# Which half chunk of the next block's weights GpSimd splits at the mixer's norm, in a decoder trunk on one Trainium2 core

## The chip, the cores and the metric

The kernel runs on one core of a Trainium2 chip. The metric is the device time of one execution in microseconds (us). Three runs of the kernel before took 1212.08, 1212.16 and 1212.49 us; their median is 1212.16.

The engines are named as in the profile: PE is TensorE (matmuls; PEld is its weight load), DVE is VectorE, ACT is ScalarE, POOL is GpSimd, and SP is SyncE, which issues most of the transfers. L180 means line 180 of the kernel.

## The reference, cut to what matters

The reference computes two layers, each with three blocks, and a layer norm behind each block. Activations are 256 tokens by 1024 features, all in float32.

```python
for l in range(DEPTH):                       # DEPTH = 2
    h = _swiglu(x, ffn_w1[l, 0], ffn_w3[l, 0], ffn_w2[l, 0])
    x = _layernorm(ALPHA * x + 0.5 * h, ln_g[l, 0], ln_b[l, 0])
    h = _mixer(x, l, w_in[l], ...)           # ends with: m @ w_out
    x = _layernorm(ALPHA * x + h, ln_g[l, 1], ln_b[l, 1])
    h = _swiglu(x, ffn_w1[l, 1], ffn_w3[l, 1], ffn_w2[l, 1])
    x = _layernorm(ALPHA * x + 0.5 * h, ln_g[l, 2], ln_b[l, 2])

def _swiglu(x, w1, w3, w2):                  # d_ff = 2816
    return (jax.nn.silu(x @ w1) * (x @ w3)) @ w2
```

The mixer is a gated pair of branches (a spatial gating unit and a differential attention), whose sum `m` goes through `w_out`. The change touches the passage from that last product, over the layer norm behind it, into the first products of the second SwiGLU of the same layer. There is one such passage in each layer, so two in all.

## The kernel before

**Products in three matmuls.** Each float32 operand is held as a hi part (rounded to the format that the matmul reads) and a lo part (what the rounding left). A product is three matmuls into one accumulator: hi weights by hi x, lo weights by hi x, hi weights by lo x (`three`, L256 is its matmul). The profile names the parts `whi`, `wlo` for weights and `x` for both parts of the new x (`mhi`, `mlo` for the operand of `w_out`).

**Weights come in chunks.** `stream` (L152) fetches one chunk of weights, 128 partitions by 2048 float32 (1 MB), by one transfer of SyncE's queue into a `raw` buffer (L163; there are four). The chunk falls into two half chunks, and each half into two pieces of 128x512. For each piece ScalarE makes the hi part (L178) and another engine makes the lo part by subtracting it from the raw weights (L180). That engine is VectorE, except for the half chunks that the argument `pool` names, which go to GpSimd. The hi and lo buffers for half chunks come from two pools of eight each; they become free as TensorE reads the last matmul of the half chunk that held them. `lent` names half chunks that are put into spare activation buffers instead (`lhi`, `llo`), so that they can be split before the pools have room.

**The first products of a block.** `gemm_b2` (L317) multiplies the 256 tokens, as two halves of 128 (t = 0 and 1), by two weight matrices (m = 0 and 1) of 512 columns each, over 8 row tiles of 128 (c = 0 and 1 hold four each). That makes four chunks n = 2c + m. For t = 0 each is fetched, split and used for 12 matmuls; for t = 1 the same four are used again. The order of a chunk's use in t = 0 is n = 0, 1, 2, 3. Chunks 0 and the first half of 1 are lent. The second half of 1, and all of 2 and 3, are in the pools.

**The norm between.** The block before a norm ends with `gemm_b2` for `w_out`, whose first token half is complete 48 matmuls ahead of its second. `Norm.part` (L467, and L471 for statistics) adds the residual; `Norm.finish` aggregates (L478), takes a reciprocal root in one-element steps (`rsqrt`, L228 to L234), normalises the two halves of the features (L487, two pieces of 128x512), and writes the second one as two 16-bit planes (L526) for a transposing transfer. All of this is on VectorE. TensorE transposes the first feature half itself (L533). `affine` then applies the norm's gain and bias on ScalarE (L580), and `split` makes the hi and lo parts of the new x (L220 on ScalarE, L222 on VectorE; on GpSimd for the second feature half of the first tokens). The next block's first matmul needs x's parts.

**What sets the order.** TensorE's program is in the order written. The other engines' order comes from a scheduler that goes by priorities; `behind(ins)` puts an instruction behind another in that order, and the lists `after` and `lent` and the argument `pool` of `gemm_b2` are written out for the passage. `norm.ends[0]` is the last plane (L526) of the first token half, and `norm.ends[1]` that of the second. `norm.front` is the index of the norm in its layer: it is 1 only for the norm behind the mixer.

In the kernel before, at a passage behind the mixer, GpSimd makes the lo parts of the second half of chunk 2; VectorE makes the others. VectorE's lo parts for the second half of chunk 1 and the first half of chunk 2 stand behind the planes of the first token half; chunk 3's stand behind those of the second token half.

Of the kernel before, what the change touches and what calls it, by code (L numbers as in the profile page):

```python
# [54 lines left out]
def trunk(ctx, tc, x, xT, w13a, w13b, w2, wb, wqk, wu, wg, wgr, wbr, wbrr, wo, gateb, gatebr, sgug, sgub, sguwT, sgubias, lam, diffg,  # L55
# [22 lines left out]
    def bank():  # L78
        return psum.tile([P, 512], F32, tag="main", name=name("bank"))
# [68 lines left out]
    def behind(ins):  # L148

        return tc.issue_after(ins) if ins is not None else nullcontext()  # L150

    def stream(src, width=CH, sub=HC, lent=(), after=(None, None), pool=()):  # L152

        step()
        raw = raw_pool.tile([P, CH], F32, tag="raw", name=name("raw"))
        for g in gate:
            g[0] -= 1
        while len(gate) > 1 and gate[1][0] < 0:  # L160
            gate.pop(0)
        with behind(gate[0][1] if gate and gate[0][0] < 0 else None):
            loaded[0] = nc.sync.dma_start(raw[:, :width], src).ins  # L163
        out = []
        first = sooner.pop() if sooner else latest
        for o in range(0, width, HC):
            eng = G if o // HC in pool else V
            if o // HC in lent:
                hi, lo = ([act.tile([P, 512], F32R, tag="slot", name=name(n)) for _ in range(2)] for n in ("lhi", "llo"))
                at = [(hi[j], lo[j]) for j in range(2)]  # L170
            else:
                hi = hi_pool.tile([P, HC], F32R, tag="hi", name=name("whi"))
                lo = lo_pool.tile([P, HC], F32R, tag="lo", name=name("wlo"))
                at = [(hi[:, p : p + sub], lo[:, p : p + sub]) for p in range(0, HC, sub)]
            for p, (h, w) in zip(range(0, HC, sub), at):
                r = raw[:, o + p : o + p + sub]
                with behind(first[0]):
                    A.activation(h, r, AF.Copy)  # L178
                with behind(after[o // HC] or (first[1] if eng is V else None)):
                    eng.tensor_tensor(out=w, in0=r, in1=h.bitcast(F32), op=ALU.subtract)  # L180
            out.append((hi, lo))
        return out
# [104 lines left out]
    def rows_b(ps, t, k0, piece, xh, xl, kts, c0=0, n=512, first=0):  # L287

        hi, lo = piece
        for j in range(2):  # L290
            k, o = k0 + j, j * 512 + c0
            wh, wl = (w[j][:, c0 : c0 + n] if isinstance(w, list) else w[:, o : o + n] for w in (hi, lo))
            three(ps[:, :n], xh(k)[:, t * P : (t + 1) * P], xl(k)[:, t * P : (t + 1) * P], wh, wl,
                  k == first, k == (first - 1) % kts)
        beat(n / 1024)
# [21 lines left out]
    def gemm_b2(srcs, xh, xl, done, norm=None, second=(0, 1), each=None):  # L317

        lent, after = [()] * 4, [(None, None)] * 4
        if norm:
            lent = [(0, 1), (0,), (), ()]
            after[1:3] = (None, norm.ends[0]), (norm.ends[0], None if norm.front == 1 else norm.ends[0])
        ps = [[bank() for _ in range(2)] for _ in range(NT)]
        got = [[None] * 4 for _ in range(2)]
        for t in range(NT):
            order = second if t else (0, 1)
            for c in order:
                if norm:  # L330
                    norm.ready(t, c)
                    after[3] = [norm.ends[1]] * 2
                for m in range(2):
                    n = 2 * c + m
                    if t == 0:
                        got[m][2 * c : 2 * c + 2] = stream(srcs[m][:, c * CH : (c + 1) * CH], sub=512, lent=lent[n],
                                                           after=after[n], pool=(1,) if norm and norm.front == 1 and n == 2 else ())
                    for i in range(2 * c, 2 * c + 2):
                        rows_b(ps[t][m], t, 2 * i, got[m][i], xh, xl, KT, first=order[0] * KT // 2)
                    if each and c == order[1]:  # L340
                        each(t, m, ps[t][m])
            with behind(latest[0] if t == 0 else None):
                done(t, ps[t])
# [255 lines left out]
    def ffn(l, f, i, norm, last=False):  # L599
# [33 lines left out]
        for n in range(NB):  # L633
            srcs = [w13b[l, f, m * NB + n] for m in range(2)]
            if n == 0 and norm is None:
                gemm_first(srcs, front(n, (10.3, 10.3)))
            else:
                gemm_b2(srcs, xh, xl, front(n, (13.3, 10.3)), norm=norm if n == 0 else None)
# [17 lines left out]
    def mixer(l, i, norm):  # L656
# [5 lines left out]
        def got_val(t, ps):  # L662
            for h in range(2):
                with behind(norm.xhi[1, 0]):
                    A.activation(val[t][:, h], ps[h], AF.Copy)

        gemm_b2([wb[l, VAL_, 0], wb[l, VAL_, 1]], xh, xl, got_val, norm=norm)

        hb = slots("hb", 2 * KT, F32R)
# [273 lines left out]
        for c, m in branch_columns(0, ha, ((0,), (1,))):  # L943
# [3 lines left out]
        ln = Norm(l, i, 2.0 * ALPHA, 4.0 * EPS, m[:, :1])  # L947

        gemm_b2([wo[l, 0], wo[l, 1]], view(m_hi), view(m_lo), lambda t, ps: ln.finish(t, 1.9), second=(1, 0),
                each=lambda t, h, ps: ln.part(t, h * 512, ps))  # L950
        return ln.close()

    norm = None
    for l in range(DEPTH):
        norm = ffn(l, 0, 0, norm)
        norm = mixer(l, 1, norm)
        norm = ffn(l, 1, 2, norm, last=l == DEPTH - 1)
# [87 lines left out]
```

## Time and profile before

| | before |
|---|---|
| median of three runs | 1212.16 us |
| the profiled execution | 1212.03 us |
| its span, first to last instruction | 1210.3 us |
| granted TensorE clock | 1.000 |
| PE busy | 1203.2 us (99% of the span) |
| PEld busy | 1012.9 us (84%) |
| DVE busy | 905.2 us (75%) |
| ACT busy | 720.1 us (59%) |
| POOL busy | 334.9 us (28%) |

Busy time is the time in which an engine's instructions ran, whether or not anything waited for them. The chain of work that ended last is the view that tells what sets the end: it is followed back from the last instruction to what released it, step by step. In rows of the timeline the first number is the start from the span's beginning and the second the length of the row; "x2" means two instructions merged into one row, and the bracket at the end is the idle time of the engine just before the row, with what ended it. Two instructions of one engine may overlap by some hundredths of a microsecond, as the next is taken up while the last drains.

### The profile page before, as it was taken

The numbers are of one execution on the slowest core, as the hardware profiler recorded it, in microseconds if no ns is written. First come the engines' busy times: TensorE is split into PE (matmuls) and PEld (weight loads), VectorE is DVE, ScalarE is ACT, GpSimd is POOL, SyncE is SP. The second block draws the span as 40 slices with busy tenths as digits, with TensorE's granted clock in tenths as the row PEclk, the third lists the DMA queues.
The fourth block names the chain that finished last, engine by engine and source line by source line (L and its number), as shares of the span: only waits on it lengthen the run. The fifth ranks groups of instructions, "written<-read, shape, count | busy, mean of one in ns | idle before, by whom it ended". The sixth has DMA issues, their size and how long they took to land.

```text
span 1210.3 us, 16816 instructions
## 1 busy us (share of the span) xinstructions
PE 1203.2 (99%) x5891; PEld 1012.9 (84%) x5891; DVE 905.2 (75%) x1544; ACT 720.1 (59%) x1388; POOL 334.9 (28%) x442
## 2 busy tenths in 40 slices
PE   9999999999999999999999999999999999999998
PEld 8888888888888888888888888888888887888887
DVE  7676669897688986766686766688976989776763
ACT  7465547668855665554555564576698556564740
POOL 1433101156411233330053330003564012423300
PEclk9999999999999999999999999999999999999999
DMA  9977746767765566766476757476676764877540
GB/s 348 301 224 234 251 174 205 261 198 229 239 218 183 191 235 204 252 197 260 148 246 200 259 183 261 148 273 232 213 217 194 250 191 146 276 230 239 186 180 35
DMA packets 124005, 263.58 MB, mean 218 GB/s; under 512 B 88416, under 2 KB 89488, under 8 KB 97808
## 3 DMA queue, kind: packets, MB, share of 16 engines
q1 hardware_dynamic: 119664, 248.80, 61.6%
q0 software_dynamic: 3824, 13.18, 3.4%
q8 instruction: 46, 0.75, 0.2%
q10 hardware_dynamic: 432, 0.52, 0.1%
q14 instruction: 39, 0.32, 0.1%
HBM read 236.52 MB, written 1.05 MB: 196 GB/s over the span
## 4 chain that ended last, share of the span: by engine, by line
PE 95%; DVE 4%; issue 1%; ACT 0%; ACTq 0%
PE bank L256 69%; PE bank L268 15%; PE bank L275 7%; PE bank L374 2%; PE sbank L704 1%; DVE wlo L180 1%; PE sbank L760 1%; PE sbank L878 1%; DVE llo L180 1%; DVE st L471 0%; PE sbank L386 0%; DVE xtok L467 0%; DVE nvia L526 0%; PE sbank L758 0%; DVE mlo L222 0%
## 5 line engine op out<-in xcount | busy, mean ns | idle before, releaser
L180 DVE TENSOR_TENSOR wlo<-raw,whi 128x512 fp32r<-128x512 f32 (+1 forms) x566 | 526.0, 964 | 114.1 <-ACT whi L178 80.0
L178 ACT ACTIVATE whi<-raw 128x512 fp32r<-128x512 f32 (+1 forms) x570 | 433.3, 799 | 246.8 <-PE bank L256 181.0
L256 PE MATMUL bank<-whi,x 128*128 128x512 f32 x1480 | 460.6, 390 | 0.0
L256 PEld LDWEIGHTS bank<-whi,x 128*128 128x128 f32 x1480 | 277.9, 188 | 57.8
L256 PE MATMUL bank<-wlo,x 128*128 128x512 f32 x740 | 288.0, 389 | 0.0
L256 PEld LDWEIGHTS bank<-wlo,x 128*128 128x128 f32 x740 | 139.0, 188 | 28.1
L268 PE MATMUL bank<-x,whi 128*128 128x512 f32 x640 | 153.3, 391 | 0.0
L193 POOL COPY planes<-planes 128x512 uint16<-128x512 uint16 x80 | 90.4, 1157 | 190.9 <-DVE planes L613 190.9
L256 PE MATMUL bank<-whi,hhi 128*128 128x512 f32 (+1 forms) x374 | 141.2, 378 | 0.0
L256 PE MATMUL bank<-wlo,hhi 128*128 128x512 f32 (+1 forms) x374 | 141.0, 377 | 0.0
L256 PE MATMUL bank<-whi,hlo 128*128 128x512 f32 (+1 forms) x374 | 140.9, 377 | 0.0
L268 PEld LDWEIGHTS bank<-x,whi 128*128 128x128 f32 x640 | 118.2, 188 | 23.8
L202 POOL COPY planes<-planes 128x512 uint16<-128x512 uint16 x80 | 69.5, 913 | 96.2 <-DMA planes<-planes 95.8
L613 DVE TENSOR_TENSOR planes<-planes,bank 128x512 f32<-128x512 f32 x40 | 27.3, 683 | 85.8 <-issue 70.9
L612 ACT ACTIVATE planes<-bank 128x512 f32<-128x512 f32 x40 | 23.9, 598 | 103.7 <-PE bank L256 102.2
L275 PEld LDWEIGHTS bank<-x,wlo 128*128 128x128 f32 x640 | 81.4, 191 | 2.9
L275 PE MATMUL bank<-x,wlo 128*128 128x256 f32 x640 | 82.6, 283 | 0.0
L256 PEld LDWEIGHTS bank<-whi,hlo 128*128 128x128 f32 x374 | 70.4, 188 | 13.0
L256 PEld LDWEIGHTS bank<-whi,hhi 128*128 128x128 f32 x374 | 70.4, 188 | 12.8
L256 PEld LDWEIGHTS bank<-wlo,hhi 128*128 128x128 f32 x374 | 70.4, 188 | 12.6
L575 POOL COPY nvia<-ntwo 128x256 uint16<-128x256 uint16 x20 | 10.3, 563 | 195.6 <-DMA ntwo<-nvia 177.4
L680 POOL TENSOR_TENSOR swap<-swap,sin_t 128x512 f32<-128x512 f32 x16 | 25.3, 1582 | 103.2 <-DMA swap<-z 80.6
(209 smaller groups left out, 1393.4 us busy)
## 6 DMA issues: line engine op xcount, KB each, us to landing
raw<-in_w13b SPq DMA_DIRECT2D x76, 1024.0 KB, 5.8
raw<-in_w SPq DMA_DIRECT2D x40, 1024.0 KB, 6.3
raw<-in_wb SPq DMA_DIRECT2D x16, 1024.0 KB, 5.2
raw<-in_wqk SPq DMA_DIRECT2D x16, 1024.0 KB, 6.5
raw<-in_w13a SPq DMA_DIRECT2D x8, 1024.0 KB, 5.1
raw<-in_wgr SPq DMA_DIRECT2D x8, 1024.0 KB, 5.6
raw<-in_wg SPq DMA_DIRECT2D x8, 1024.0 KB, 5.2
raw<-in_wu SPq DMA_DIRECT2D x8, 1024.0 KB, 6.4
```

Source lines behind the costliest of these rows:

```text
L178: A.activation(h, r, AF.Copy)
L180: eng.tensor_tensor(out=w, in0=r, in1=h.bitcast(F32), op=ALU.subtract)
L193: G.tensor_copy(out=planes(out)[:, w], in_=numbers(src)[:, w])
L202: eng.tensor_copy(out=numbers(out)[:, w], in_=planes(src)[:, w])
L256: PE.matmul(ps, xx, w, start=start and n == 0, stop=stop and n == 2)
L268: PE.matmul(b[-1], hi[:, k * P : (k + 1) * P], xc(k), start=k == 0, stop=False)
L275: PE.matmul(b[n][:, :T], lo[:, k * P : (k + 1) * P], xc(k)[:, :T], start=False, stop=k == KT - 1)
L374: PE.matmul(ps[t][m], x[:, j, o + t * P : o + (t + 1) * P], y, start=k0 + j == 0 and o == 0 and y is hi, stop=k0 + j == KT - 1 and y is lo)
L612: silu[0] = A.activation(s, ps[0], AF.Silu).ins
L613: added[0] = V.tensor_tensor(out=s, in0=s, in1=ps[1], op=ALU.mult).ins
L680: turned_by[0] = G.tensor_tensor(out=s3, in0=s3, in1=s, op=ALU.mult).ins
L704: PE.matmul(banks[m][:, j * nk : (j + 1) * nk], rows(qT, m, j, t * P, P), rows(kT, m, j, 0, nk), start=True, stop=True)
```

## The change

At the passage behind the mixer, GpSimd makes the lo parts of the second half of chunk 1 in place of the second half of chunk 2. They carry no order of their own: they stand where they may run as soon as their hi parts and their buffer are there. The second half of chunk 2 goes to VectorE, behind the planes of the first token half. At the other norms (`norm.front` 0 and 2) the new lists say the same as the old ones, and nothing changes.

```diff
         if norm:
             lent = [(0, 1), (0,), (), ()]
-            after[1:3] = (None, norm.ends[0]), (norm.ends[0], None if norm.front == 1 else norm.ends[0])
+            after[1:3] = (None, None if norm.front == 1 else norm.ends[0]), [norm.ends[0]] * 2
...
                     if t == 0:
                         got[m][2 * c : 2 * c + 2] = stream(srcs[m][:, c * CH : (c + 1) * CH], sub=512, lent=lent[n],
-                                                           after=after[n], pool=(1,) if norm and norm.front == 1 and n == 2 else ())
+                                                           after=after[n], pool=(1,) if norm and norm.front == 1 and n == 1 else ())
```

In the built program this moves two instructions on VectorE and two on GpSimd at each passage. VectorE's two lo parts for the second half of chunk 1, first behind the planes, are gone, and two for the second half of chunk 2 stand behind those for its first half. GpSimd's pair keeps its place in GpSimd's order, between the loads of the next norm's gain and bias (L434) and its plane copies (L575), and now reads chunk 1. TensorE's order is the same; its two matmuls with chunk 1's lo parts of that half now wait for GpSimd. ScalarE's order and SyncE's are the same.

## The prediction, made before the change was run

> **What bounds the kernel now.** I read the page's chain of work first, then the same chain in order of time, then TensorE's own rows where that chain leaves TensorE.
>
> ```profile
> PE 95%; DVE 4%; issue 1%; ACT 0%; ACTq 0%
> 398.84 0.53 issue
> ...
> 416.13 1.41 issue
> 417.54 1.84 DVE nvia L526 x2
> 419.38 2.41 DVE wlo L180 x4
> ...
> 423.11 0.60 DVE x L222
> 423.75 108.65 PE bank L256 x478
> ...
> 997.29 0.53 issue
> ...
> 1022.46 108.64 PE bank L256 x478
> ```
>
> 95% of the end is TensorE; what an edit off TensorE can win is only the time in which TensorE stands. The chain leaves TensorE for long at two places, 398.84 to 423.75 us and 997.29 to 1022.46 us: the two passages from a mixer to the FFN behind it (layers 0 and 1), which are the places this diff touches. There the norm of the first token half runs on VectorE: normalise (L487 x2), planes (L526 x2), four weight lo parts (L180 x4), then the lo part of the new x (L222), for which TensorE waits.
>
> TensorE at the first passage (columns: start, length, line, out<-in; a matmul starts when the array takes it, so steps are read from start to start):
>
> ```profile
> 417.56 0.39 PE L256 MATMUL bank<-whi,mlo 128*128 128x512 f32 x1
> ...
> 418.15 0.48 PE L256 MATMUL bank<-whi,mhi 128*128 128x512 f32 x1
> ...
> 422.59 0.39 PE L256 MATMUL bank<-llo,x 128*128 128x512 f32 x1
> 423.75 0.73 PE L256 MATMUL bank<-lhi,x 128*128 128x512 f32 x2 [0.78 <-DVE x L222]
> 424.32 0.39 PE L256 MATMUL bank<-llo,x 128*128 128x512 f32 x1
> ...
> 427.52 0.39 PE L256 MATMUL bank<-whi,x 128*128 128x512 f32 x1
> ...
> 434.32 0.39 PE L256 MATMUL bank<-lhi,x 128*128 128x512 f32 x1
> ```
>
> From 427.52 to 434.32 lie 30 matmuls (6 of the ordinary half of chunk 1, 12 each of chunks 2 and 3): 6.80/30 = 0.227 us a step. From 422.59 to 424.32 lie three steps, 0.68 undisturbed, and they take 1.73: 1.05 lost. From 424.32 to 434.32 lie 44 steps, 9.97 at that rate, in 10.00: 0.03 more lost in a slow restart.
>
> The second passage:
>
> ```profile
> 1016.01 0.39 PE L256 MATMUL bank<-whi,mlo 128*128 128x512 f32 x1
> 1016.38 0.66 PE L533 MATMUL sbank<-ident,xtok 128*128 128x128 f32 x4
> 1016.79 0.48 PE L256 MATMUL bank<-whi,mhi 128*128 128x512 f32 x1
> ...
> 1021.21 0.39 PE L256 MATMUL bank<-llo,x 128*128 128x512 f32 x1
> 1022.46 0.73 PE L256 MATMUL bank<-lhi,x 128*128 128x512 f32 x2 [0.86 <-DVE x L222]
> 1023.03 0.39 PE L256 MATMUL bank<-llo,x 128*128 128x512 f32 x1
> ```
>
> Here 1021.21 to 1023.03 is 1.82, less 0.68: 1.14 lost. And the four transposes (L533) start late: 1016.01 to 1016.79 is 0.78 where the first passage has 0.59 (417.56 to 418.15), 0.19 lost waiting for the normalised half.
>
> **The change, part by part.** Chunk n is the n-th of the four weight chunks of the block; each has two half chunks, each of two 128x512 lo parts. Both kernels give GpSimd two lo parts a passage, and VectorE the rest; every engine keeps its count, ScalarE and SyncE their order, so no DMA is added or moved past another. VectorE now makes the second half of chunk 2 where it made the second half of chunk 1: same four L180 behind the planes, no cost. GpSimd's two lo parts go from chunk 2 to chunk 1. The rows that matter (L178 makes the hi parts on ScalarE):
>
> ```profile
> 412.55 1.15 ACT L178 ACTIVATE whi<-raw 128x512 fp32r<-128x512 f32 x2 [3.16 <-PE bank L256]
> ...
> 415.33 1.15 ACT L178 ACTIVATE whi<-raw 128x512 fp32r<-128x512 f32 x2 [0.22 <-PE bank L256]
> ...
> 420.42 0.64 ACT L220 ACTIVATE x<-xf 128x512 fp32r<-128x512 f32 x1
> ```
> ```profile
> 416.04 2.71 POOL L180 TENSOR_TENSOR wlo<-raw,whi 128x512 fp32r<-128x512 f32 x2 [9.48 <-ACT whi L178]
> 1014.49 2.97 POOL L180 TENSOR_TENSOR wlo<-raw,whi 128x512 fp32r<-128x512 f32 x2 [9.10 <-ACT whi L178]
> ```
>
> The first hi row is chunk 1's second half, the second chunk 2's second half (chunk 2's first is between them). GpSimd starts 0.71 behind its hi part (415.33 to 416.04) and has been idle for 9.48, so it is the hi part alone that holds it. Behind chunk 1's it starts at 412.55 + 0.71 = 413.26, 2.78 earlier, and ends 2.71 to 2.97 later, at 415.97 to 416.23.
>
> What that does to VectorE is read from the rows in which the two ran together and one in which they did not:
>
> ```profile
> 415.50 2.11 DVE L487 TENSOR_SCALAR xtok<-xtok,mv,nwy 128x512 f32<-128x512 f32 x2
> 415.97 1.65 DVE L487 TENSOR_SCALAR xtok<-xtok,mv,nwy 128x512 f32<-128x512 f32 x1
> 417.54 1.50 DVE L526 COPY nvia<-xtok 128x512 uint16<-128x512 uint16 x1
> 418.96 0.42 DVE L526 COPY nvia<-xtok 128x512 uint16<-128x512 uint16 x1
> 427.35 0.55 DVE L487 TENSOR_SCALAR xtok<-xtok,mv,nwy 128x512 f32<-128x512 f32 x1
> 427.93 0.43 DVE L526 COPY nvia<-xtok 128x512 uint16<-128x512 uint16 x1
> ```
>
> Alone (427.35, 427.93) a normalise takes 0.55 and a plane 0.43. Under GpSimd's first lo part the second normalise takes 1.65, under its second lo part the first plane 1.50, ending at 419.04, which is 0.29 after GpSimd ended (416.04 + 2.71 = 418.75). The second plane, behind it, is back at 0.42. So VectorE's wide one-input operations stand until GpSimd's is through. With GpSimd done at 415.97 to 416.23, only the first normalise (415.50) is touched: it ends 0.29 behind, at 416.26 to 416.52. The second follows 0.47 later (the spacing 415.97 - 415.50), the planes 0.46 (0.03 gap and 0.43) and 0.34 (419.38 - 419.04) later: 417.53 to 417.79, against 419.38 now, 1.6 to 1.85 earlier.
>
> The Trainium skill, "SBUF — State Buffer", section "Who interferes with whom", says that of a VectorE operation in a two-port mode and a GpSimd one, the first to issue holds the shared ports for its whole instruction and the other blocks fully; by that rule, and the trace agrees with its 1.65 and 1.50, the order matters and not the mean load.
>
> L222 moves with it from 423.11 to 421.26 to 421.51. Its hi part is ready at 420.42 + 0.64 = 421.06, so ScalarE does not hold it, and it is through 0.64 later (423.11 to 423.75), by 421.9 to 422.15. TensorE asks for it at 422.59 + 0.23 = 422.82. The wait goes wholly, with 0.7 to 0.9 to spare. The second passage has the same instructions in the same order, with GpSimd's pair 598.45 later (1014.49) and TensorE's request 598.62 later (1021.21 against 422.59): I take the same 1.6 to 1.85, more than the 1.14 lost there, and the transposes find their half, worth the 0.19.
>
> What is late next: GpSimd's lo part has a new reader, a TensorE wait, at 427.52, 11 us behind its end: nothing. Chunk 2's second half, now VectorE's, is ready about 420 and is asked for at 430.2 (427.52 and 12 steps): nothing. GpSimd's next work waits for a transpose that starts when the planes end, and comes earlier with them.
>
> Sum: 1.05 + 0.03 at the first passage, 1.14 + 0.02 (taken like the first's) + 0.19 at the second: 2.43 us. Behind both, the chain is TensorE's again (108.65 and 108.64 at one stretch), which carries the gain on. The profiled execution takes 1212.03 (span 1210.3): 1209.60. It is 0.13 below the median of the three runs, 1212.16, so I forecast 1209.7. About what a measurement of this kernel can tell from no change is 0.2%, 2.42 us, a bound at 1209.74: my sum lies on it.
>
> The cost that before does not show is VectorE's small operations (the eight one-element steps of the root, 413.45 to 415.50) beside GpSimd's 128x512 lo parts. The nearest row is GpSimd's own L222:
>
> ```profile
> 424.60 1.57 POOL L222 TENSOR_TENSOR x<-nvia,x 128x256 fp32r<-128x256 f32 x2 [1.50 <-ACT x L220]
> ...
> 425.68 0.27 DVE L233 TENSOR_SCALAR nwa<-yi,ve 128x1 f32<-128x1 f32 x1
> ...
> 413.45 0.15 DVE L228 TENSOR_SCALAR ve<-mv 128x1 f32<-128x1 f32 x1
> ...
> 413.83 0.28 DVE L233 TENSOR_SCALAR nwa<-yi,ve 128x1 f32<-128x1 f32 x1
> ```
>
> Beside GpSimd (424.60 to 426.17) the root's step takes 0.27, without it 0.28: I take nothing. The lower end is nothing too, since none of these steps waits for GpSimd now; the upper end is full blocking (third rival).
>
> **The rivals.** First, the wait comes back at the second token half, whose x is asked for at 434.32:
>
> ```profile
> 423.62 0.68 DVE L467 SCALAR_TENSOR_TENSOR xtok<-xtok,bank 128x512 f32<-128x512 f32 x1
> ...
> 434.51 0.39 ACT L220 ACTIVATE x<-nvia 128x256 fp32r<-128x256 f32 x1
> ```
>
> That half's norm begins with L467 at 423.62. Its last matmul is two steps ahead of 422.59 and through 0.39 later, at 422.5, so VectorE is what holds it and it moves up by about a microsecond too; then nothing is lost. Were something else to hold it (a transpose, ScalarE), x's third column tile, ready at 434.90, would be asked for six steps behind the earlier head, 434.32 - 1.08 + 1.36 = 434.60: 0.30 lost, and 0.57 at the second passage by the same sum with 1.35 for 1.08. That gives 1209.73 + 0.87 = 1210.6.
>
> Second, GpSimd does not start early and nothing moves: 1212.2. Against it: it idles 9.48, and its buffer belongs to the half chunk whose hi buffer came free at 412.55.
>
> Third, the other side: GpSimd's lo parts block the small steps as they block the wide ones. The eight steps (413.45 to 415.50, 2.05) would start at about 416.0 and normalise at 418.0; the two pairs, now alone, take 1.82 (0.47 + 0.55, 0.03 + 0.43 + 0.34): 419.8, 0.45 behind now. Transposes and x follow: 0.9 over both passages, 1213.1; over 1214.6 only if GpSimd's parts get longer by it as well. It decides against the change once the steps lose more than the 1.85 won. The skill's page, same section, lists tensor_scalar among those that can take the two-port mode, which speaks for it; the 0.27 speaks against.
>
> **How the numbers follow.** Forecast 0.82: 1209.5 to 1210.1, since the runs of before spread over 0.4; a little over half of it beyond the bound, 0.48 against 0.34. First rival 0.09, second 0.03, both within 0.2%. Third 0.06: 0.02 within, 0.04 beyond. Faster 0.48, same 0.48, slower 0.04. The range takes in the forecast with 0.5 below it for slow steps that I have not counted, and the first rival with as much again as it costs, 1209.0 to 1211.3; it leaves out the last two cases and little more.
>
> **What would show it.** GpSimd's L180 at about 413.3 and 1011.7; the second normalise near 0.55 and both planes near 0.43; the root's steps at 0.15 to 0.28 still; L222 at 421.3 to 421.5; TensorE from the llo matmul at 422.59 to the next in 0.23; no new wait near 433. The prediction is wrong if the root's steps grow, if a TensorE gap reappears at the second half's head, or if GpSimd's L180 still starts at 416.

## The result, and the profile after

The changed kernel took 1209.74 us in the median of 21 runs (1209.36 to 1210.40). The kernel before took 1212.42 in as many runs on the same chips (1210.73 to 1212.93), 0.26 above the three runs shown ahead of the prediction. The ratio is 0.998, with a 95% interval of 0.9973 to 0.9986: 2.68 us, 0.22%. That is just beyond the 0.2% that the prediction took as the bound, but the interval, 0.14% to 0.27%, takes the bound in. The profiled execution took 1210.00, with a span of 1208.3.

The chain of work in order of time, of the changed kernel, at the first passage and then at the second (start, length, what; the views end at 440 and 1030, and with them the last row of each):

```profile
400.58 17.71 PE bank L256 x78
418.30 0.44 PE sbank L533 x4
418.73 21.36 PE bank L256 x94
...
998.03 17.71 PE bank L256 x78
1015.74 0.44 PE sbank L533 x4
1016.18 13.88 PE bank L256 x61
```

VectorE, which carried most of this chain from 398.84 to 423.75 before, is no longer in it. TensorE's own rows at the place where it stood 1.05 us, and then at the same place of the second passage:

```profile
422.93 0.39 PE L256 MATMUL bank<-llo,x 128*128 128x512 f32 x1
423.15 0.62 PE L256 MATMUL bank<-lhi,x 128*128 128x512 f32 x2
423.61 0.39 PE L256 MATMUL bank<-llo,x 128*128 128x512 f32 x1
...
433.58 0.39 PE L256 MATMUL bank<-lhi,x 128*128 128x512 f32 x1
...
1020.37 0.39 PE L256 MATMUL bank<-llo,x 128*128 128x512 f32 x1
...
1021.05 0.39 PE L256 MATMUL bank<-llo,x 128*128 128x512 f32 x1
```

Three steps in 0.68 at both, and no gap at the head of the second token half either: 47 steps from 422.93 to 433.58, 0.227 each. What made it so, on ScalarE, GpSimd and VectorE (timeline of the changed kernel, engine by engine):

```profile
412.89 1.15 ACT L178 ACTIVATE whi<-raw 128x512 fp32r<-128x512 f32 x2 [2.77 <-PE bank L256]
...
413.61 2.55 POOL L180 TENSOR_TENSOR wlo<-raw,whi 128x512 fp32r<-128x512 f32 x2 [6.31 <-ACT whi L178]
...
414.18 0.15 DVE L228 TENSOR_SCALAR ve<-mv 128x1 f32<-128x1 f32 x1
...
416.24 1.00 DVE L487 TENSOR_SCALAR xtok<-xtok,mv,nwy 128x512 f32<-128x512 f32 x2
417.15 0.75 DVE L526 COPY nvia<-xtok 128x512 uint16<-128x512 uint16 x2
417.83 2.49 DVE L180 TENSOR_TENSOR wlo<-raw,whi 128x512 fp32r<-128x512 f32 x4
...
421.56 0.68 DVE L222 TENSOR_TENSOR x<-xf,x 128x512 fp32r<-128x512 f32 x1
422.90 0.69 DVE L467 SCALAR_TENSOR_TENSOR xtok<-xtok,bank 128x512 f32<-128x512 f32 x1 [0.67 <-PE bank L256]
```

GpSimd's pair is through at 416.16, before VectorE's first wide operation (416.24). The two normalises take 1.00 together instead of 2.11, the two planes 0.75 instead of 1.84. L222 is through at 422.24, 0.9 ahead of TensorE's request (422.93 + 0.23), and VectorE now waits 0.67 for TensorE at L467: the wait has turned round.

### The profile page after: what moved, and what is told of

Its sections match the earlier page's. It is cut to its first block, busy times and chain, and to the rows that moved or that the text cites. A ratio compares the mean times of both kernels' runs of the same rounds, so it can differ in the third digit from the quotient of the medians.

```text
span 1208.3 us, 16816 instructions
## 1 busy us (share of the span) xinstructions
PE 1202.6 (100%) x5891; PEld 1013.3 (84%) x5891; DVE 903.2 (75%) x1544; ACT 719.9 (60%) x1388; POOL 332.9 (28%) x442
## 3 DMA queue, kind: packets, MB, share of 16 engines
HBM read 236.52 MB, written 1.05 MB: 197 GB/s over the span
## 4 chain that ended last, share of the span: by engine, by line
PE 99%; DMA 0%; DVE 0%; ACT 0%; issue 0%; ACTq 0%
PE bank L256 72%; PE bank L268 15%; PE bank L275 8%; PE bank L374 2%; PE sbank L704 1%; PE sbank L760 1%; PE sbank L878 1%; DMA xraw<-in_xT 0%; PE sbank L758 0%; PE sbank L533 0%; PE sbank L512 0%; DVE xtok L520 0%; ACT whi L220 0%; DVE st L471 0%; DVE xtok L467 0%; ACT x L220 0%
## 5 line engine op out<-in xcount | busy, mean ns | idle before, releaser
L202 POOL COPY planes<-planes 128x512 uint16<-128x512 uint16 x80 | 70.9, 931 | 95.8 <-DMA planes<-planes 95.5
L575 POOL COPY nvia<-ntwo 128x256 uint16<-128x256 uint16 x20 | 10.4, 565 | 198.1 <-DMA ntwo<-nvia 179.9
```

What stands on the lines that cost most here:

```text
L202: eng.tensor_copy(out=numbers(out)[:, w], in_=planes(src)[:, w])
```

## The experiments

The theory: VectorE's wide operations stand while GpSimd's weight lo parts run; the change takes GpSimd out of their way, and TensorE gets back what it lost there. The main rivals: it is VectorE's load that counts, or the choice of the half chunk as such. Each kernel below is timed against the kernel before on the same chip, which took 1212.38 us in the median beside the first four below and 1212.63 beside the others.

**GpSimd takes no lo parts.** VectorE makes all six behind the planes.

```diff
-            after[1:3] = (None, None if norm.front == 1 else norm.ends[0]), [norm.ends[0]] * 2
+            after[1:3] = (None, norm.ends[0]), [norm.ends[0]] * 2
...
-   pool=(1,) if norm and norm.front == 1 and n == 1 else ())
+   pool=())
```

> GpSimd makes no weight lo parts at the two passages; VectorE makes all six behind the planes, two more than in either kernel. Theory (VectorE's wide one-input operations stand while GpSimd works; with the overlap gone they take 0.55 and 0.43): the planes end as early as in the changed kernel, two more lo parts cost 1.2 us, L222 ends about 0.3 behind TensorE's request, so a stall of 0.3 to 0.4 a passage: 1210.3 to 1210.6 us. Rival (what counts is the load on VectorE, and GpSimd's help shortens the chain): two more lo parts on the chain put x 1.2 us later than before at each passage: about 1214.8 us.

Measured: 1210.36 us, ratio 0.9984 (0.9975 to 0.9993). VectorE, then TensorE, in its timeline:

```profile
415.94 1.00 DVE L487 TENSOR_SCALAR xtok<-xtok,mv,nwy 128x512 f32<-128x512 f32 x2
416.86 0.76 DVE L526 COPY nvia<-xtok 128x512 uint16<-128x512 uint16 x2
417.53 3.69 DVE L180 TENSOR_TENSOR wlo<-raw,whi 128x512 fp32r<-128x512 f32 x6
...
422.47 0.68 DVE L222 TENSOR_TENSOR x<-xf,x 128x512 fp32r<-128x512 f32 x1
...
422.64 0.39 PE L256 MATMUL bank<-llo,x 128*128 128x512 f32 x1
423.20 0.73 PE L256 MATMUL bank<-lhi,x 128*128 128x512 f32 x2 [0.17 <-DVE x L222]
423.77 0.39 PE L256 MATMUL bank<-llo,x 128*128 128x512 f32 x1
```

VectorE does 1.2 us more than in the kernel before and x comes earlier all the same; TensorE loses 1.13 - 0.68 = 0.45 here, and as much at the second passage. In the kernel before, GpSimd's help cost more than the work it took over. The rival's 1214.8 is out.

**GpSimd works on into the old time.** As the changed kernel, with its two lo parts made twice.

```diff
+            if eng is G:
+                for p, (h, w) in list(zip(range(0, HC, sub), at))[:again]:
+                    G.tensor_tensor(out=w, in0=raw[:, o + p : o + p + sub], in1=h.bitcast(F32), op=ALU.subtract)
             out.append((hi, lo))
...
-   pool=(1,) if norm and norm.front == 1 and n == 1 else ())
+   pool=(1,) if norm and norm.front == 1 and n == 1 else (), again=2)
```

> As the changed kernel, but GpSimd makes its two lo parts of chunk 1 a second time into the same buffer, so that it works on from 416.2 to about 418.7 as it did before. Theory: the second normalise (or the first) and the first plane stand again, the planes end near 419.7, the whole wait of TensorE is back: 1212.0 to 1212.8 us. Rival (the gain comes from which half chunk goes to GpSimd: its hi parts, its buffers): nothing comes back, 1209.6 to 1209.9 us.

Measured: 1212.20 us, ratio 1.0 (0.9991 to 1.0009). GpSimd, VectorE and TensorE (its lines stand three later, L490 for L487):

```profile
416.06 2.71 POOL L183 TENSOR_TENSOR wlo<-raw,whi 128x512 fp32r<-128x512 f32 x2
...
416.19 2.87 DVE L490 TENSOR_SCALAR xtok<-xtok,mv,nwy 128x512 f32<-128x512 f32 x2
418.99 0.75 DVE L529 COPY nvia<-xtok 128x512 uint16<-128x512 uint16 x2
...
417.85 0.39 PE L259 MATMUL bank<-whi,mlo 128*128 128x512 f32 x1
419.12 0.66 PE L536 MATMUL sbank<-ident,xtok 128*128 128x128 f32 x4 [0.87 <-DVE xtok L490]
419.53 0.48 PE L259 MATMUL bank<-whi,mhi 128*128 128x512 f32 x1
```

The gain is gone with the half chunk unchanged, so the half chunk as such wins nothing. This time both normalises stand and no plane, and TensorE loses its time at the transposes (419.53 - 417.85 = 1.68 where 0.59 is undisturbed, 1.09) instead of at x, where 0.05 is left: nearly the same delay, asked for elsewhere.

**Half of that.** The same with `again=1`.

> As the changed kernel, but GpSimd makes one of its two lo parts a second time, so that it works to about 417.5. Theory: one wide operation stands, about 1.1 us on VectorE's chain, of which 0.9 is the slack that the changed kernel has at L222; 0.2 to 0.3 of stall with the restart a passage: 1210.1 to 1210.5 us. Rival (each blocked operation costs its full length, no slack): 2.1 us for both passages, about 1211.9 us.

Measured: 1210.12 us, ratio 0.9982 (0.9973 to 0.9991).

```profile
416.10 1.48 POOL L183 TENSOR_TENSOR wlo<-raw,whi 128x512 fp32r<-128x512 f32 x1
...
415.73 2.14 DVE L490 TENSOR_SCALAR xtok<-xtok,mv,nwy 128x512 f32<-128x512 f32 x2
```

The normalises take 2.14 for 1.00, the 1.1 us expected, and the rival's 1211.9 is out: the slack takes it up. TensorE shows no long step at the first passage in this profile and 0.15 at the second (0.70 for 0.59 at the transposes, 0.72 for 0.68 at x), less than the 0.2 to 0.3 expected at each. The median stands 0.38 above the changed kernel's; 0.15 of it is read here, and the rest, inside this run's interval of about 1.1 us to each side, stays open.

**The first passage alone, the second alone.** The norm keeps its layer, and the change is made only where the layer is 0 (shown), or 1.

```diff
+            if norm.front == 1 and norm.layer != 0:
+                after[1:3] = (None, norm.ends[0]), (norm.ends[0], None)
+            else:
+                after[1:3] = (None, None if norm.front == 1 else norm.ends[0]), [norm.ends[0]] * 2
...
+   pool=(1,) if norm and norm.front == 1 and n == (1 if norm.layer == 0 else 2) else ())
```

> The change at the first passage alone, the second as before. Theory: the first passage's 1.08 us of the 2.43 are won, 1211.3 us against 1212.4; TensorE's long step stays at the second passage and is gone at the first. Rival (the two passages share one cause further on and only both together win anything): 1212.4 us, with a new wait behind the first passage.

Measured: 1210.97 us, ratio 0.9991 (0.9982 to 0.9999), 1.41 won where 1.08 was counted.

> The change at the second passage alone. The first passage alone won 1.4 us where 1.08 had been counted from the profile of before. Theory: the profile of before caught VectorE early at its first passage (GpSimd's copies L202 near 399 us held it less than in the later profiles), so the usual loss there is about 1.4; the second passage then wins the rest of 2.68, about 1.3: 1211.1 us, and this run's own first passage shows a loss of 1.3 to 1.5 us. Rival (the two passages do not add up, winning one makes the other smaller): 1211.3 us or more, and the first passage loses 1.05 as in the profile of before.

Measured: 1211.07 us, ratio 0.9989 (0.9980 to 0.9998). Against the 1212.4 that this expectation reckoned with that is 1.3; against its own chip's 1212.63 it is 1.56. The two passages together give 2.7 to 3.0 for the 2.68 of the whole change. Each of the two times has an interval of about 1.1 us to each side, so they can't separate the expected 1211.1 from the rival's 1211.3; the traces do. TensorE at the unchanged first passage of this run:

```profile
417.38 0.39 PE L256 MATMUL bank<-whi,mlo 128*128 128x512 f32 x1
...
418.16 0.48 PE L256 MATMUL bank<-whi,mhi 128*128 128x512 f32 x1
...
422.56 0.39 PE L256 MATMUL bank<-llo,x 128*128 128x512 f32 x1
423.83 0.73 PE L256 MATMUL bank<-lhi,x 128*128 128x512 f32 x2 [0.88 <-DVE x L222]
424.40 0.39 PE L256 MATMUL bank<-llo,x 128*128 128x512 f32 x1
```

Read as in the prediction: 1.84 - 0.68 = 1.16 at x and 0.78 - 0.59 = 0.19 at the transposes, 1.35 where the first profile had 1.05. At the changed second passage nothing is lost. In the run with the first passage changed it is the other way round: nothing at the first, 1.36 at the second.

**The kernel before, profiled again.**

> The kernel before once more, for a second profile of it. Theory: the losses of TensorE at the passages are not fixed; at the first one 1.3 to 1.5 us where the first profile had 1.05, at the second 1.3 to 1.5. Rival: 1.05 and 1.33 again, and the 0.25 us by which the measured gain passes the counted one comes from elsewhere.

One run, 1213.04 us. TensorE at its first passage:

```profile
418.20 0.39 PE L256 MATMUL bank<-whi,mlo 128*128 128x512 f32 x1
...
418.99 0.48 PE L256 MATMUL bank<-whi,mhi 128*128 128x512 f32 x1
...
423.43 0.39 PE L256 MATMUL bank<-llo,x 128*128 128x512 f32 x1
...
425.24 0.40 PE L256 MATMUL bank<-llo,x 128*128 128x512 f32 x1
```

0.20 and 1.13, 1.33. Read the same way, the unchanged second passages of three profiles show 1.33 (the first profile), 1.36 (this one) and 1.36 (the first passage alone changed). So the first profile's first passage, with 1.05, was the odd one of six. The two first passages differ already 20 us earlier. In this profile GpSimd's copies (L202) hold VectorE's pair of lo parts and the next operation, 0.5 each; in the first one they came earlier and the pair alone was held, 0.64 (1.29 is the pair's time undisturbed, below):

```profile
400.33 2.12 POOL L202 COPY gr<-gr 128x512 uint16<-128x512 uint16 x2 [6.29 <-ACT whi L178]
...
400.02 1.81 DVE L180 TENSOR_TENSOR wlo<-raw,whi 128x512 fp32r<-128x512 f32 x2 [0.53 <-issue]
401.75 1.19 DVE L222 TENSOR_TENSOR mlo<-gate,mhi 128x512 fp32r<-128x512 f32 x1
```

The first profile of the kernel before:

```profile
398.93 1.89 POOL L202 COPY gr<-gr 128x512 uint16<-128x512 uint16 x2 [5.45 <-DMA gr<-gr]
...
399.38 1.93 DVE L180 TENSOR_TENSOR wlo<-raw,whi 128x512 fp32r<-128x512 f32 x2 [0.53 <-issue]
401.23 0.68 DVE L222 TENSOR_TENSOR mlo<-gate,mhi 128x512 fp32r<-128x512 f32 x1
```

In the second profile the root's first step (L228) comes 1.03 later (414.48 for 413.45) and TensorE's last matmul before its wait 0.84 later (423.43 for 422.59). So VectorE is 0.19 later against TensorE, which would make up most of the 0.28 between 1.05 and 1.33; that this is the whole cause is not shown.

**The old half chunk, later.** The kernel before, GpSimd's pair behind its plane copies.

```diff
                 if norm:
                     norm.ready(t, c)
+                    if t == 0 and c == 1 and norm.front == 1:
+                        after[2] = norm.ends[0], behind_norm[0]
```

> The kernel before, with GpSimd's two lo parts of the same half chunk as there (the second of chunk 2) moved behind its plane copies L575, to about 421.5 to 424.2, when VectorE is through its normalise and planes. VectorE's order is that of before. Theory (the overlap is what costs): 1209.6 to 1210.2 us, the small excess for GpSimd's lo part of x, which now waits behind. Rival (the half chunk whose hi parts come first is what wins): 1212.4 us.

Measured: 1209.82 us, ratio 0.9977 (0.9967 to 0.9986), the changed kernel's time with the old half chunk (its lines stand two later, L489 for L487).

```profile
421.17 3.00 POOL L180 TENSOR_TENSOR wlo<-raw,whi 128x512 fp32r<-128x512 f32 x2
...
415.83 1.00 DVE L489 TENSOR_SCALAR xtok<-xtok,mv,nwy 128x512 f32<-128x512 f32 x2
...
421.57 1.45 DVE L222 TENSOR_TENSOR x<-xf,x 128x512 fp32r<-128x512 f32 x1
```

Ahead of VectorE's wide operations or behind them is the same to TensorE. Here GpSimd holds L222 instead (1.45 for 0.68), and the slack covers it: L222 is through at 423.02, TensorE's matmul behind it starts at 423.23.

**GpSimd's copies near 399 us write only.** The kernel before, two copies replaced by a memset, as its expectation tells.

```diff
-            joined(g, p, G)
+            joined(g, p, G) if t == 0 else G.memset(p, 0.0)
```

> The kernel before, with the two copies of GpSimd near 399 and 998 us (L202 on the second token half, which put the transposed planes together again) replaced by one memset of the same tile at the same place, which reads nothing; so the mixer's first 512 columns of the second token half are left out, and the output is not the reference's. Theory (VectorE's operations with two operands in SBUF also stand while GpSimd reads): the pair of lo parts there takes 1.29 instead of 1.8 to 1.9 and the next lo part 0.69 instead of up to 1.19, so VectorE comes 0.6 to 1.0 us earlier and TensorE's loss shrinks by as much at each passage: 1210.3 to 1211.1 us. Rival (that stretch has room, since VectorE then waits for TensorE's sums anyway): 1212.4 us.

Measured: 1209.72 us, ratio 0.9977 (0.9968 to 0.9986).

```profile
399.62 0.53 POOL L918 MEMSET gr<- 128x512 f32 x1 [6.12 <-DMA gr<-gr]
...
416.25 4.13 POOL L180 TENSOR_TENSOR wlo<-raw,whi 128x512 fp32r<-128x512 f32 x1 [10.13 <-ACT whi L178]
...
399.59 1.29 DVE L180 TENSOR_TENSOR wlo<-raw,whi 128x512 fp32r<-128x512 f32 x2 [0.53 <-issue]
400.80 0.69 DVE L222 TENSOR_TENSOR mlo<-gate,mhi 128x512 fp32r<-128x512 f32 x1
...
415.14 1.00 DVE L487 TENSOR_SCALAR xtok<-xtok,mv,nwy 128x512 f32<-128x512 f32 x2
416.06 0.75 DVE L526 COPY nvia<-xtok 128x512 uint16<-128x512 uint16 x2
416.74 2.49 DVE L180 TENSOR_TENSOR wlo<-raw,whi 128x512 fp32r<-128x512 f32 x4
```

The durations near 400 came as expected (1.29, 0.69). The median is 0.58 or more better than expected. The interval reaches up to 1210.9, into the expected range, so the time alone doesn't settle it, but TensorE's rows do: its steps at x take 0.68 at both passages and those at the transposes 0.59 and 0.58, so the whole loss is gone, and not a part of it. VectorE is earlier, so that its normalise (415.14) starts 1.11 ahead of GpSimd (416.25), where it was 0.54 ahead in the first profile (415.50, 416.04), and GpSimd no longer gets in. Now GpSimd stands: its first lo part takes 4.13 us, through at 420.38, 1.15 behind the end of VectorE's four lo parts (419.23). At the second passage it is the same: VectorE is 1.10 ahead (1012.57, 1013.67), and GpSimd's pair takes 5.39, as it does at the first. So the rival is out, and so is the half of the theory that reckoned with a shift at unchanged blocking.

## Why the prediction was right, and where it was off

The direction, the mechanism and the time (1209.7, measured 1209.74) held. By its steps:

- **GpSimd's early start** held: 0.72 behind its hi part (412.89 to 413.61; 0.71 was taken). It took 2.55 and not 2.71 to 2.97, as at every passage where it ran beside the root's small steps.
- **The first normalise touched** failed here, harmlessly: the prediction took VectorE's 415.50 from the first profile, and VectorE came at 416.24, 0.08 behind GpSimd's end, so that pair and planes took 1.00 and 0.75. Where only the first passage was changed, VectorE came 0.42 ahead of GpSimd's end (415.96, 416.38). There the first normalise took 0.71 and ended 0.29 behind GpSimd, just as the prediction had it, and TensorE lost nothing either.
- **The root's small steps take nothing** held: 2.06 us (414.18 to 416.24) wholly or nearly under GpSimd's pair, 2.05 before. The third rival, which hung on them, is out.
- **L222 with 0.7 to 0.9 to spare** held: 0.9.
- **Nothing late next** held: no gap at 433.58, against the first rival, and none at the matmuls that now wait for GpSimd.
- **The sum** was short, 2.43 for 2.68. The term that was mis-sized is "1.05 + 0.03 at the first passage". One profile was taken for the kernel, and it had caught VectorE early. Two later profiles of the same passage show 1.33 and 1.35, read the same way; with that the sum is 2.71 to 2.73.
- **The median** moved too: more runs of before put it 0.26 higher. The forecast 1209.7 came true because both ends of the difference were short by about a quarter of a microsecond: that it fits to 0.04 us is luck; the direction and the mechanism are not. Which side of 0.2% the result would fall on, the prediction could not tell.

The Trainium skill, "SBUF — State Buffer", section "Who interferes with whom", says that a VectorE operation with two operands in SBUF contends with a GpSimd one that reads SBUF and not with one that only writes it. The traces agree: VectorE's pair of lo parts and L222 took 1.81 and 1.19 beside GpSimd's copies (400.33 to 402.45). The memset (399.62 to 400.15) ran beside the first of the pair, and the pair took 1.29, as two lo parts do elsewhere in that profile (2.49 for four); L222, behind the memset's end, took 0.69. So the writing side rests on one overlap of 0.53 a passage.

## What to carry to other kernels

When VectorE's chain ends a wait of TensorE, look at what GpSimd runs at that time: help that overlaps the chain's wide operations can cost more than it takes over (here all six lo parts on VectorE beat the shared work by 2.0 us). Move the helper's work to where VectorE does one-element steps, waits, or no longer matters; which of the two half chunks it was did not count here (1209.74 and 1209.82). And size a stall of a microsecond from more than one profile.

## What had not been expected

An operation of GpSimd can stand for several of VectorE's in a row. In the last experiment one lo part, 1.28 alone (2.55 for two), took 4.13. It stood through VectorE's remaining plane and all four two-operand lo parts, and got in only about when VectorE fell idle; the prediction reckoned with waits for a single operation. In the kernel before, it was the other way round: GpSimd came during the normalises, got in behind the first of them (its first lo part took 1.29 to 1.58 at the four passages profiled), and VectorE stood. About half a microsecond in arrival, made by GpSimd's own copies some 16 us earlier, decided which of the two engines stood, and with it the whole gain. That GpSimd is kept out for the whole row of operations is read from the two passages of one run, where it came during the planes; what would let it in between was not tried.
